# A trunk of two layers on one core: the opening in two parts of 512 features

## The chip, the cores and the metric

One core of a Trainium2 chip. The metric is device time in microseconds of one execution; three executions of the kernel before took 1212.24, 1216.07 and 1216.48 us, so the median is 1216.07. The engines are told by their plain names: TensorE (PE in the profile; PEld its weight loads), VectorE (DVE), ScalarE (ACT), GpSimd (POOL) and SyncE (SP), whose queue issues nearly all DMAs.

## The reference

A residual stream x of 256 tokens by 1024 features, float32, goes through two layers of three sub-layers. Each sub-layer takes a shift, a scale and a gate of 1024 features from one conditioning vector c, by c @ mod_w + mod_b, and computes

```
y = f(x * (1 + scale) + shift)
x = layer_norm(alpha * x + (1 + gate) * y)        # the feed-forwards enter with half the step
```

The first and the last sub-layer of a layer are feed-forwards, f(u) = (silu(u @ w_gate) * (u @ w_up)) @ w_down, with 2816 columns between; the middle one mixes tokens (sparse attention beside a gated delta rule in the first layer, latent attention in the second). Only the input of the first feed-forward, u = x * (1 + scale) + shift, and that feed-forward's first products are touched here.

## The kernel before, in words

All products that need float32 are made of three products of rounded parts: `split` (line 257) makes the high part on ScalarE (a cast, line 258) and the low part by a subtraction on VectorE or GpSimd (line 259); `mm3` adds high x high, high x low, low x high in PSUM (lines 263 to 265). u is kept transposed, features on partitions, as eight tiles of 128 features by 256 tokens, high and low.

The first feed-forward goes over 11 chunks of 256 of its 2816 columns. A chunk has two tiles of 128 columns; each needs a gate and an up product over all eight feature tiles, 96 matrix products per chunk. Behind chunk c come the down products of the two tiles of chunk c - 1 (12 products of 512 columns for each tile), so that TensorE has work while the silu of a chunk is made. Weights of a chunk come as two DMAs of 1 MB into tiles with the tag `w8` (three buffers); a down tile and a tile of modulation weights are 0.5 MB each with the tag `wd` (three buffers, shared). The low parts of the first eight down tiles are made on GpSimd (`load_down`, line 455), the rest on VectorE. `pace` draws modulation tiles in step with the chunks: from the fourth tile of columns on, those of the first gate (summed by VectorE, line 225, then over partitions by TensorE, line 180), then those of the next sub-layer.

The opening, ahead of the first chunk, has this order in SyncE's queue: c, the scale's weights (four DMAs of 1 MB), x (1 MB), the shift's weights (three of 1 MB, two of 0.5 MB), then the first chunk's gate and up weights in four pieces of 128 columns (512 bytes a row), then down tiles 0 and 1 and chunk 1. VectorE adds up weight rows times c over the eight row tiles (lines 218 and 225); TensorE sums over partitions by products with a column of ones (`mod_cols0`, line 147). One of the shift's eight tiles goes to TensorE directly. x is transposed by TensorE into PSUM as soon as it is there, and a few products with no use (`warm`) keep TensorE busy. When B, the shift with its bias, is there, VectorE and ScalarE make u pair by pair of feature tiles (`make_u`), and the first chunk's products follow in a written-out order of its parts (line 540). All of u needs all of the scale and the shift: 9 MB stand ahead of the first product.

The order of instructions on an engine is set by the tile framework: it follows the order of the program, but may take a later instruction first where it reckons that an earlier one is still waiting. `behind(...)` holds what is written in its block behind marked instructions of the same engines.

Of the kernel before, what the change touches and what calls it, by code (L numbers as in the profile page):

```python
# [30 lines left out]
HYBRID_LATE, LATENT_LATE = (1,), (5,)  # of these rows, the second block's products come last  # L31


class Trunk:
# [48 lines left out]
    def setup_bias(self):  # L83
        """the biases of shift and scale, as columns"""
# [36 lines left out]
    def warm(self, a):  # L121
        """keeps the PE array's clock up while nothing else can run on it"""
# [8 lines left out]
    def mod_cols(self, acc):  # L131
        """sum of acc over its partitions, [column % 128, column // 128]"""
# [9 lines left out]
    def mod_cols0(self, acc, c, use=None):  # L142
        """the same by products with c, which start earlier; use: takes two columns at a time"""
        pts = [self.bank("gu", (P, KD)) for _ in range(2 if use else 1)]
        for k in range(KD):
            pt = pts[k // 2 % len(pts)]
            self.last_col = self.nc.tensor.matmul(pt[:, k : k + 1], acc[:, k * P : (k + 1) * P], c,
                                                  start=True, stop=True)
            if use and k % 2:
                use(slice(k - 1, k + 1), pt)  # L150
        return pts[0]

    def mod_scale(self, si, sums):
# [4 lines left out]
        if si:  # L158
            l, j = self.subs[si - 1]
            o = (l * 3 + j) * KD  # L160
            nc.vector.tensor_tensor(out=B, in0=A, in1=self.pcol[:, 48 + o : 48 + o + KD], op=ALU.mult)
            nc.vector.tensor_tensor(out=A, in0=A, in1=self.pcol[:, o : o + KD], op=ALU.mult)
        self.AB[si] = [A, B]

    def mod_shift(self, si, acc):
# [3 lines left out]
        if si == 0:  # L169
            self.mod_cols0(acc, self.one[:, 0:1], lambda c, pt: add(B[:, c], pt[:, c], B[:, c]))  # L170
        else:
            add(B, B, b)
            add(B, B, self.mod_cols(acc))

    def mod_gate(self, si, acc, G):
        """G holds the bias"""
# [8 lines left out]
    def mod_gen(self):  # L185
        """(c @ mod_w + mod_b) of every sub-layer, in the order of use; partition sums come last; yields tiles loaded"""
        nc, t = self.nc, self.t
        self.AB, self.G = {}, {}
        todo = [(si, i, k) for si in range(len(self.subs)) for i in (1, 0, 2) for k in range(KD)]
        ws, loaded, G, step = {}, 0, None, None  # L190

        def load(si, i, k):
# [3 lines left out]
            if si or i == 2 or (i == 0 and k >= KD - 2):  # L196
                ws[si, i, k] = self.tl(self.wp, [P, D], "wd", bufs=3)
                nc.sync.dma_start(ws[si, i, k], src)
            elif k % 2 == 0:
                w2 = self.tl(self.wp, [P, 2, D], "w8", bufs=3)  # L200
                src = t["mod_w"][l, k * P : (k + 2) * P, off : off + D]
                nc.sync.dma_start(w2, src.rearrange("(q p) f -> p q f", p=P))
                ws[si, i, k], ws[si, i, k + 1] = w2[:, 0], w2[:, 1]

        for n, (si, i, k) in enumerate(todo):
            if k == 0:
                l, j = self.subs[si]
                off = (j * 3 + i) * D
                acc = self.tl(self.wp, [P, D], "G", bufs=2) if si == 0 and i < 2 else self.tl(self.wp, [P, D], "macc")
# [7 lines left out]
            if k == 0:  # L217
                nc.vector.tensor_scalar_mul(acc, w, c)
            elif (si, i, k) == (0, 0, 5):
                self.share = self.mod_cols0(w, c)  # L220
                with self.behind(self.last_col):
                    for _ in range(2):
                        self.warm(self.x[:, 0, 0:512])
            else:
                step = nc.vector.scalar_tensor_tensor(acc, w, c, acc, ALU.mult, ALU.add)  # L225
# [3 lines left out]
            self.mod_sums(si, i, acc, G, step)  # L229
            self.mdone.add((si, i))  # L230
            yield 0
            if si == 0 and i == 1:
                self.setup_bias()
                self.load_x()

    def mod_sums(self, si, i, acc, G, step):
        if i == 2:
            self.mod_gate(si, acc, G)
        elif i == 1:
            if si:  # L240
                self.mod_scale(si, self.mod_cols(acc))
            else:
                self.scale = self.mod_cols0(acc, self.one[:, 0:1])
        else:
            if not si:
                with self.behind(step):
                    self.mod_scale(si, self.scale)
                    self.nc.vector.tensor_tensor(out=self.AB[0][1], in0=self.share[:, 0:KD], in1=self.bcol[:, 0, 0],
                                                 op=ALU.add)
# [19 lines left out]
    def make_u(self, si, n, blocks):  # L269
        """n [P, NB, D] tokens on partitions -> uT = n * A + B, hi and lo [P, 2, KD, S]; blocks: one or all of them"""  # L270
        nc = self.nc
        if 0 in blocks:
            self.u = self.tl(self.wp, [P, 2, KD, S], "uT", F32R)
        u = self.u
        W = len(blocks) * P
        joint = len(blocks) > 1

        def rows(k0):
            pt = self.bank("acc" if joint else "gu", (P, 2, W))
            for q in range(2):  # L280
                for c, b in enumerate(blocks):
                    nc.tensor.transpose(pt[:, q, c * P : (c + 1) * P], n[:, b, (k0 + q) * P : (k0 + q + 1) * P],
                                        self.ident)
            return pt

        def affine(k0, pt):
            A, B = self.AB[si]
            ts = slice(blocks[0] * P, blocks[0] * P + W)
            if joint and k0 > 2:
                v = vs[:, k0 // 2 - 2]  # L290
            else:
                v = self.tl(self.wp, [P, 2, W], "tmp" if joint else "v", bufs=2 if joint else 3)
            for q, k in enumerate((k0, k0 + 1)):
                a, b = A[:, k : k + 1], B[:, k : k + 1]
                if q == 0 and (joint or blocks[0]):
                    nc.vector.tensor_scalar(v[:, q], pt[:, q], a, b, ALU.mult, ALU.add)
# [1206 lines left out]
```

## Time and profile before

| | |
|---|---|
| three executions | 1212.24, 1216.07, 1216.48 us |
| span of the profiled execution | 1212.3 us |
| TensorE busy | 1135.4 us, 94% |
| VectorE busy | 905.5 us, 75% |
| ScalarE busy | 547.6 us, 45% |
| GpSimd busy | 255.4 us, 21% |
| moved by DMA | 259.76 MB, 214 GB/s on the mean |

The span is the time from the first to the last instruction of one profiled execution; the profile gives no other time for that execution. Busy time of TensorE is modelled from pipelined matmuls, so that two products that start 0.12 us apart are each shown with 0.28 us; starts, not durations, tell its pace. A wait is put down to the engine that came last before the waiting instruction started.

### The profile page before, as it was taken

Reading aid. Unit: us, or ns where it says so; the run is one execution under the profiler, and the core shown is the slowest. Engines: PE = TensorE matmul, PEld = TensorE weight load, DVE = VectorE, ACT = ScalarE, POOL = GpSimd, SP = SyncE. Lnnn points to the kernel's source line nnn. Section 1 sums busy time; section 2 is a strip of 40 time slices with the busy share of each in tenths; the row PEclk is TensorE's granted clock in tenths of the full one; section 3 lists DMA queues with packets and bytes.
Section 4 is the critical chain, followed back from the end, with each engine's and each line's share of the span. In section 5 each row is a group of like instructions: output and inputs, shape, how many; then the busy total and the mean of one; then the engine's idle time right before and its main releaser. Section 6 shows DMA issues by size and latency. Waiting matters only on the chain.

```text
span 1212.3 us, 19687 instructions
## 1 busy us (share of the span) xinstructions
PE 1135.4 (94%) x7783; PEld 1035.5 (85%) x7783; DVE 905.5 (75%) x1376; ACT 547.6 (45%) x959; POOL 255.4 (21%) x186
## 2 busy tenths in 40 slices
PE   4998999999899998999999899899989998999997
PEld 3897999788787887989999889799978878899995
DVE  6699777698985677878885888778788438866545
ACT  0644444456433445533543543334456556544430
POOL 0631000224731452320000322000221234300001
PEclk9999999999999999999999999999999998999999
DMA  9779999454310586788997488889725135876620
GB/s 352 249 260 345 303 319 303 145 165 123 98 36 5 188 274 212 243 291 297 325 307 238 139 283 284 269 297 302 266 79 168 66 105 180 295 250 189 215 72 35
DMA packets 155334, 259.76 MB, mean 214 GB/s; under 512 B 8813, under 2 KB 117354, under 8 KB 155242
## 3 DMA queue, kind: packets, MB, share of 16 engines
q1 hardware_dynamic: 155050, 258.45, 63.9%
q8 instruction: 61, 1.00, 0.3%
q14 instruction: 31, 0.25, 0.1%
q10 hardware_dynamic: 192, 0.05, 0.0%
HBM read 257.43 MB, written 1.05 MB: 213 GB/s over the span
## 4 chain that ended last, share of the span: by engine, by line
PE 51%; DVE 22%; DMA 13%; ACT 5%; issue 5%; POOL 3%; SPq 0%; POOLq 0%; DVEq 0%; ACTq 0%
PE gu L265 8%; PE gu L264 8%; PE gu L263 7%; DMA wd<-ffn_w_down 7%; PE acc L265 6%; PE acc L263 6%; PE acc L264 6%; DVE macc L225 3%; DMA wd<-mod_w 3%; DMA w<-ffn_w_up 2%; DVE g L259 2%; POOL hd L259 2%; PE gu L732 2%; DVE u L259 2%; ACT hd L258 1%
## 5 line engine op out<-in xcount | busy, mean ns | idle before, releaser
L225 DVE SCALAR_TENSOR_TENSOR macc<-wd,csT,macc 128x1024 f32<-128x1024 f32 x112 | 169.0, 1509 | 27.1 <-DMA wd<-mod_w 26.5
L263 PE MATMUL gu<-uT,g 128*128 128x256 f32 x640 | 181.1, 283 | 1.4 <-ACT sg L548 1.4
L265 PE MATMUL gu<-uT,g 128*128 128x256 f32 x640 | 181.2, 283 | 1.2 <-DVE g L259 1.2
L265 PE MATMUL gu<-uT,u 128*128 128x256 f32 x640 | 181.2, 283 | 1.0 <-DVE u L259 1.0
L263 PE MATMUL gu<-uT,u 128*128 128x256 f32 x640 | 181.1, 283 | 0.0
L264 PE MATMUL gu<-uT,u 128*128 128x256 f32 x640 | 181.1, 283 | 0.0
L264 PE MATMUL gu<-uT,g 128*128 128x256 f32 x640 | 181.1, 283 | 0.0
L258 ACT CAST hd<-wd 128x1024 fp32r<-128x1024 f32 x88 | 92.2, 1049 | 136.8 <-DMA wd<-ffn_w_down 118.9
L263 PE MATMUL acc<-hd,h 128*128 128x512 f32 x352 | 141.3, 401 | 1.5 <-ACT h L258 1.5
L265 PE MATMUL acc<-hd,h 128*128 128x512 f32 x352 | 137.6, 391 | 1.1 <-DVE h L259 1.1
L264 PE MATMUL acc<-hd,h 128*128 128x512 f32 x352 | 137.7, 391 | 0.0
L259 DVE TENSOR_TENSOR g<-w,g 128x1024 fp32r<-128x1024 f32 x86 | 118.9, 1386 | 22.8 <-ACT g L258 22.3
L263 PEld LDWEIGHTS gu<-uT,g 128*128 128x128 f32 x640 | 122.7, 192 | 3.2 <-ACT sg L548 1.8
L265 PEld LDWEIGHTS gu<-uT,g 128*128 128x128 f32 x640 | 122.7, 192 | 1.6 <-DVE g L259 1.6
L264 PEld LDWEIGHTS gu<-uT,g 128*128 128x128 f32 x640 | 122.7, 192 | 1.4
L265 PEld LDWEIGHTS gu<-uT,u 128*128 128x128 f32 x640 | 122.9, 192 | 1.2 <-DVE u L259 1.2
L263 PEld LDWEIGHTS gu<-uT,u 128*128 128x128 f32 x640 | 122.9, 192 | 0.0
L264 PEld LDWEIGHTS gu<-uT,u 128*128 128x128 f32 x640 | 122.9, 192 | 0.0
L259 DVE TENSOR_TENSOR u<-w,u 128x1024 fp32r<-128x1024 f32 x81 | 104.1, 1290 | 24.5 <-ACT u L258 24.3
L258 ACT CAST u<-w 128x1024 fp32r<-128x1024 f32 (+1 forms) x89 | 91.6, 1039 | 62.7 <-DMA w<-ffn_w_up 51.9
L259 POOL TENSOR_TENSOR hd<-wd,hd 128x1024 fp32r<-128x1024 f32 x32 | 86.6, 2712 | 141.6 <-ACT hd L258 141.6
L259 POOL TENSOR_TENSOR hl<-w,hl 128x1024 fp32r<-128x1024 f32 x28 | 72.5, 2602 | 202.2 <-ACT hl L258 201.7
(392 smaller groups left out, 2495.2 us busy)
## 6 DMA issues: line engine op xcount, KB each, us to landing
wd<-mod_w SPq DMA_DIRECT2D x130, 512.0 KB, 4.8
wd<-ffn_w_down SPq DMA_DIRECT2D x88, 512.0 KB, 4.6
w<-ffn_w_gate SPq DMA_DIRECT2D x43, 1024.0 KB, 8.3
w<-ffn_w_up SPq DMA_DIRECT2D x43, 1024.0 KB, 6.9
w<-hyb_w_in SPq DMA_DIRECT2D x16, 1024.0 KB, 6.1
w<-mod_w SPq DMA_DIRECT2D x7, 1024.0 KB, 7.5
w<-hyb_w_out SPq DMA_DIRECT2D x4, 1024.0 KB, 4.9
w<-mla_w_out SPq DMA_DIRECT2D x4, 1024.0 KB, 5.4
```

Of the source, the lines that this page charges most:

```text
L225: step = nc.vector.scalar_tensor_tensor(acc, w, c, acc, ALU.mult, ALU.add)
L258: i = self.nc.scalar.copy(hi, src)
L259: return i, (eng or self.nc.vector).tensor_tensor(out=lo, in0=src, in1=hi.bitcast(F32), op=ALU.subtract)
L263: nc.tensor.matmul(out, lh, rh, start=first, stop=False)
L264: nc.tensor.matmul(out, lh, rl, start=False, stop=False)
L265: self.last_mm = nc.tensor.matmul(out, ll, rh, start=False, stop=last)
L732: nc.tensor.matmul(pt[:, b * S : (b + 1) * S], q[:, b * P : (b + 1) * P], k, start=True, stop=True)
```

## The change

The opening works on features 0 to 511 first, then on 512 to 1023. For each half: the scale's weights over these 512 columns (two DMAs of 1 MB, each with four row tiles), this half of x, the shift's weights over the same columns. The sums, the products with ones, the transposes of x, A, B and four tiles of u are made per half. Between the shift's two DMAs the weights of a chunk over this half's 512 features are loaded: chunk 0 in the first half, chunk 1 in the second. Behind the second half's sums both chunks' weights over features 512 to 1023 are loaded into tiles of `w8`. Products come in four blocks of 48: chunk 0 over the first half, chunk 1 over the first half, chunk 0 over the second, chunk 1 over the second. A chunk's four sums lie in two banks of PSUM, gate and up of a tile side by side; so both tiles of a chunk are complete together. Low parts of the weights are made on GpSimd, but for the gate's second halves (VectorE). TensorE's operations of the second half (the product with ones for the scale, the transposes) are held behind the first block of products. The first modulation tiles no longer pass through `mod_gen`, no tile of the shift goes to TensorE, the bias is fetched ahead of all, and of the warming products two are left. The first sub-layer's branch of `make_u` goes. In the feed-forward of the first sub-layer, chunks 0 and 1 take their products from `opening`. All else in the diff is names and comments.

```
+    def open(self, hf, after, first, second):
+        cols, ks = slice(hf * 512, hf * 512 + 512), slice(4 * hf, 4 * hf + 4)
+        A, B = self.AB[0]
+        for i in (1, 0):
+            acc = self.open_acc[i][:, cols]
+            for q in range(2):
+                if q and not i:
+                    first()
+                r = self.tl(self.wp, [P, 4, 512], "w8", bufs=3)
+                src = t["mod_w"][0, q * 512 : (q + 1) * 512, i * D + hf * 512 : i * D + hf * 512 + 512]
+                nc.sync.dma_start(r, src.rearrange("(q p) f -> p q f", p=P))
+                for k in range(4):
+                    c = self.cs[:, 4 * q + k : 4 * q + k + 1]
+                    if q or k:
+                        nc.vector.scalar_tensor_tensor(acc, r[:, k], c, acc, ALU.mult, ALU.add)
+                    else:
+                        nc.vector.tensor_scalar_mul(acc, r[:, k], c)
+            if i:
+                nc.sync.dma_start(self.x[:, :, cols], t["x"][0][:, cols].rearrange("(b p) d -> p b d", p=P))
             else:
+                second()
+            pt = self.bank("acc", (P, 4))
+            with self.behind(*after):
+                for k in range(4):
+                    nc.tensor.matmul(pt[:, k : k + 1], acc[:, k * P : (k + 1) * P], self.one[:, 0:1], start=True, stop=True)
+            if i:
+                nc.vector.scalar_tensor_tensor(A[:, ks], pt, 1.0, self.bcol[:, 0, 1, ks], ALU.add, ALU.add)
+                turned = []
+                for k0 in range(4 * hf, 4 * hf + 4, 2):
+                    px = self.bank("acc", (P, 2, S))
+                    turned.append((k0, px))
+                    with self.behind(*after):
+                        for q in range(2):
+                            for b in range(NB):
+                                nc.tensor.transpose(px[:, q, b * P : (b + 1) * P],
+                                                    self.x[:, b, (k0 + q) * P : (k0 + q + 1) * P], self.ident)
+                        if not hf:
+                            self.warm(self.x[:, 0, 0:512])
+            else:
+                nc.vector.tensor_tensor(out=B[:, ks], in0=pt, in1=self.bcol[:, 0, 0, ks], op=ALU.add)
+        for k0, px in turned:
+            v = self.tl(self.wp, [P, 2, S], "tmp", bufs=2)
+            nc.vector.tensor_scalar(v[:, 0], px[:, 0], A[:, k0 : k0 + 1], B[:, k0 : k0 + 1], ALU.mult, ALU.add)
+            nc.scalar.activation(v[:, 1], px[:, 1], AF.Identity, scale=A[:, k0 + 1 : k0 + 2], bias=B[:, k0 + 1 : k0 + 2])
+            self.marks[1:] = self.split(self.u[:, 0, k0 : k0 + 2], self.u[:, 1, k0 : k0 + 2], v)
...
+    def opening(self, wg, wu, gp):
...
+        def load(c, hf):
+            if hf:
+                both = self.tl(self.wp, [P, 2, 4, 256], "w8", bufs=3)
+            for g, w in enumerate((wg, wu)):
+                r = both[:, g] if hf else self.tl(self.wp, [P, 4, 256], "wd", bufs=3)
+                src = w[hf * 512 : hf * 512 + 512, c * 256 : (c + 1) * 256]
+                nc.sync.dma_start(r, src.rearrange("(k p) f -> p k f", p=P))
+                hls[c, hf, g] = hl = self.tl(gp, [P, 2, 4, 256], "gu"[g], F32R)
+                self.split(hl[:, 0], hl[:, 1], r, None if hf and not g else nc.gpsimd)
+
+        def products(c, hf):
+            if not hf:
+                pts[c] = [self.bank("gu", (P, 2, S)) for _ in range(2)]
+            for kp in (0, 2):
+                for q in range(3):
+                    for s in range(2):
+                        for g in range(2):
+                            for k in (kp, kp + 1):
+                                self.last_mm = nc.tensor.matmul(
+                                    pts[c][s][:, g], hls[c, hf, g][:, q // 2, k, s * P : (s + 1) * P], u[:, q % 2, 4 * hf + k],
+                                    start=not (hf or k or q or g), stop=hf == 1 and q == 2 and k == 3, skip_group_check=True)
+
+        self.setup_bias()
+        self.open(0, (), lambda: load(0, 0), lambda: None)
+        products(0, 0)
+        self.open(1, (self.last_mm,), lambda: load(1, 0), lambda: [load(0, 1), load(1, 1)])
+        products(1, 0)
+
+        def rest(c):
+            products(c, 1)
+            return {(s, g): pts[c][s][:, g] for s in range(2) for g in range(2)}
+
+        return rest
```

## Rows read from the trace of the kernel before

**Rows 1.** The page, part 4: shares by engine of the chain that ended last.

```profile
PE 51%; DVE 22%; DMA 13%; ACT 5%; issue 5%; POOL 3%; SPq 0%; POOLq 0%; DVEq 0%; ACTq 0%
```

**Rows 2.** TensorE's waits, 0 to 240: who waited for whom, us, times, longest us.

```profile
PE gu L147 <- DVE G L225: 15.0, 1, 15.0
PE gu L180 <- DVE macc L225: 4.2, 1, 4.2
...
PE gu L265 <- DVE g L259: 1.2, 1, 1.2
```

**Rows 3.** Timeline of the opening, all engines: start, duration (us), engine, line, count.

```profile
6.42 0.75 DVE L218 TENSOR_SCALAR G<-w,csT 128x1024 f32<-128x1024 f32 x1 [3.20 <-DMA w<-mod_w]
...
17.98 3.57 PE L147 MATMUL gu<-one,G 128*128 128x1 f32 x16 [14.96 <-DVE G L225]
...
25.87 0.34 PEld L147 LDWEIGHTS gu<-csT,w 128*128 128x128 f32 x1 [0.52 <-DMA w<-mod_w]
...
26.96 2.61 DVE L225 SCALAR_TENSOR_TENSOR G<-wd,csT,G 128x1024 f32<-128x1024 f32 x2
...
30.52 1.84 PE L147 MATMUL gu<-one,G 128*128 128x1 f32 x16
...
31.06 0.16 DVE L168 TENSOR_TENSOR B<-gu,B 128x2 f32<-128x2 f32 x1 [1.35 <-PE gu L147]
...
33.62 0.80 PE L540 MATMUL gu<-uT,g 128*128 128x256 f32 x2
```

**Rows 4.** Groups by line, 0 to 34: count, busy us, mean ns, idle before.

```profile
L225 DVE SCALAR_TENSOR_TENSOR G<-w,csT,G 128x1024 f32<-128x1024 f32 x11 | 14.1, 1285 | 2.4 <-DMA w<-mod_w 2.2
```

**Rows 5.** Timeline of TensorE: around 59.7, 64.9 and 76.4.

```profile
59.73 0.48 PE L265 MATMUL acc<-hd,h 128*128 128x512 f32 x1
...
64.86 0.28 PE L263 MATMUL gu<-uT,g 128*128 128x256 f32 x1
...
76.37 0.40 PE L263 MATMUL acc<-hd,h 128*128 128x512 f32 x1
```

**Rows 6.** Timeline of VectorE, 63 to 70.

```profile
63.66 2.36 DVE L259 TENSOR_TENSOR g<-w,g 128x1024 fp32r<-128x1024 f32 x2 [0.37 <-ACT g L258]
...
68.89 3.42 DVE L225 SCALAR_TENSOR_TENSOR macc<-wd,csT,macc 128x1024 f32<-128x1024 f32 x1
```

**Rows 7.** Timeline of SyncE's queue, 22 to 66.

```profile
54.64 0.33 SPq L198 DMA_DIRECT2D wd<-mod_w  x1
...
56.17 0.40 SPq L442 DMA_DIRECT2D w<-ffn_w_gate  x1
```

**Rows 8.** Waits of SyncE's queue, 20 to 70.

```profile
SPq L198 <- POOL hd L259: 8.2, 2, 6.5
```

**Rows 9.** Timeline of GpSimd, 36 to 70.

```profile
38.86 2.42 POOL L259 TENSOR_TENSOR g<-w,g 128x1024 fp32r<-128x1024 f32 x1 [1.47 <-ACT g L258]
...
51.21 5.76 POOL L259 TENSOR_TENSOR hd<-wd,hd 128x1024 fp32r<-128x1024 f32 x2 [4.03 <-ACT hd L258]
...
68.55 2.67 POOL L259 TENSOR_TENSOR hd<-wd,hd 128x1024 fp32r<-128x1024 f32 x1 [8.07 <-ACT hd L258]
```

**Rows 10.** Timeline of ScalarE, 61 to 64.

```profile
62.58 2.00 ACT L258 CAST g<-w 128x1024 fp32r<-128x1024 f32 x2 [1.74 <-DMA w<-ffn_w_gate]
```

**Rows 11.** Timeline of VectorE, 102 to 103.5.

```profile
102.64 0.68 DVE L182 SCALAR_TENSOR_TENSOR G<-gu,G 128x512 f32<-128x512 f32 x1
```

**Rows 12.** Stretches: length, busy us (x) of PE, PEld, DVE, ACT, POOL, clock, DMA, GB/s.

```profile
46.00:60.00 14.00, 12.80 (x104) 12.37 (x103) 8.92 (x9) 6.57 (x10) 6.94 (x3) 1.00 0.63 227
...
80.00:90.00 10.00, 8.98 (x67) 8.43 (x66) 9.96 (x11) 3.53 (x5) 6.23 (x35) 1.00 0.48 147
```

**Rows 13.** The same view, behind the wait of 4.2 us.

```profile
98.00:100.00 2.00, 1.01 (x2) 0.53 (x3) 1.86 (x4) 0.69 (x2) 0.00 (x0) 0.75 1.08 350
100.00:102.00 2.00, 2.00 (x5) 0.96 (x3) 0.91 (x2) 1.91 (x2) 0.00 (x0) 0.50 1.09 367
```

**Rows 14.** The same view, as the last modulation tiles and the first weights load.

```profile
24.00:26.00 2.00, 2.00 (x8) 1.48 (x7) 1.93 (x3) 0.00 (x0) 0.00 (x0) 1.00 1.04 416
...
28.00:30.00 2.00, 2.00 (x11) 1.38 (x11) 1.68 (x4) 0.12 (x1) 0.00 (x0) 1.00 1.21 291
```

More of the change, by code (lines that the diff above doesn't have):

```diff
@@ L218, in mod_gen @@
                 nc.vector.tensor_scalar_mul(acc, w, c)
[L219 to L223, printed above, removed]
             else:
-                step = nc.vector.scalar_tensor_tensor(acc, w, c, acc, ALU.mult, ALU.add)
+                nc.vector.scalar_tensor_tensor(acc, w, c, acc, ALU.mult, ALU.add)
             yield 1
@@ L239, in mod_sums @@
         elif i == 1:
[L240 to L243, printed above, removed]
-        else:
[L245 to L249, printed above, removed]
+            self.mod_scale(si, self.mod_cols(acc))
+        else:
             self.mod_shift(si, acc)
@@ L266, in mm3, with make_u @@
         return self.last_mm
-    def make_u(self, si, n, blocks):
+    def make_u(self, si, n, b):
         nc = self.nc
-        if 0 in blocks:
+        if b == 0:
             self.u = self.tl(self.wp, [P, 2, KD, S], "uT", F32R)
         u = self.u
[L275 to L279, printed above, removed]
+        A, B = self.AB[si]
+        ts = slice(b * P, (b + 1) * P)
+        for k0 in range(0, KD, 2):
+            pt = self.bank("gu", (P, 2, P))
@@ L280, in rows @@
             for q in range(2):
[L281 to L290, printed above, removed]
-            else:
[L292 to L296, printed above, removed]
-                else:
-                    nc.scalar.activation(v[:, q], pt[:, q], AF.Identity, scale=a, bias=b)
-            self.marks[1:] = self.split(u[:, 0, k0 : k0 + 2, ts], u[:, 1, k0 : k0 + 2, ts], v)
@@ L301, in make_u @@
-        if joint:
-            pts = [rows(k0) for k0 in range(0, KD, 2)]
-            vs = self.tl(self.wp, [P, 2, 2, W], "macc")
-            self.warm(n[:, 0, 0:512])
-            while self.count < 2 * KD:
-                self.count += next(self.bg)
-            next(self.todo[0])
-            self.need(si, 0)
-            with self.behind(self.last_col):
-                for _ in range(2):
-                    self.warm(n[:, 0, 0:512])
-            for k0 in range(0, KD, 2):
-                with self.behind(self.marks[1]):
-                    affine(k0, pts[k0 // 2])
-                if k0 < 4:
-                    with self.behind(self.marks[1]):
-                        self.marks[1:] = self.between[k0 // 2]()
-        else:
-            for k0 in range(0, KD, 2):
-                affine(k0, rows(k0))
@@ L527, in ffn @@
                 else:
-                    pts = {(s, g): self.bank("gu", (P, S)) for s in r2 for g in r2}
-                    if c:
+                    if c < 2 and not ahead:
+                        pts = part(c)
+                    else:
+                        pts = {(s, g): self.bank("gu", (P, S)) for s in r2 for g in r2}
                         for s in r2:
@@ L558, in ffn @@
                         load_down(i)
-                    with self.behind(*[part] if c == 1 else after):
+                    with self.behind(*[made] if c == 1 else after):
                         self.pace(max(0, i + 1 - skip) / (NT - 2 - skip))
@@ L562, in ffn @@
                 if c > 1 and self.left is not None:
-                    with self.behind(part):
+                    with self.behind(made):
                         next(self.left, None)
@@ L811, in run @@
         self.setup()
[L812 removed]
+        self.lead, self.count = 0, 2 * KD
+        self.AB, self.G, self.mdone = {}, {}, {(0, 0), (0, 1)}
         self.bg = self.mod_gen()
[L814 to L817 removed]
+        todo = [self.sublayer(si, l, j) for si, (l, j) in enumerate(subs)]
         self.rest = self.setup_rest()
```

115 lines of the change are left out of this document (35 added, 80 removed).

## The prediction

> **What bounds the kernel now.** I read the page first, then TensorE's waits, then the timeline of the opening engine by engine, then SyncE's queue. The chain that ended last is half TensorE [rows 1]: TensorE sets the pace nearly everywhere, and what it doesn't do while it waits is what the kernel can lose or win. Its waits in the first 240 us are few [rows 2]: one of 15.0 us at the very start, behind VectorE's sums of the modulation; one of 4.2 us for the sum of the first gate (line 180); some of 1 us. So the first feed-forward, once begun, runs from 33.62 us [rows 3] with hardly a gap, and the change touches only what lies ahead of that and the two chunks behind it. In the opening the transfers lead: the first megabyte is in at 6.42 us, the eighth (seven of mod_w, one of x) at 25.87 [rows 3], so 19.45 / 7 = 2.78 us a megabyte. VectorE sums at the same rate: two passes of 1.285 us a megabyte [rows 4], 2.6 us. The last sum ends at 29.57; the products of the shift's columns start at 30.52, behind warming products; the first two columns of B are done at 31.22; the first product of the feed-forward starts 2.40 us later [rows 3]. Chunk 1's products end at about 59.7, the rest of the first two down tiles takes until 64.86, and then chunk 2 starts [rows 5], just as its first low part is ready (63.66 + 2.36 / 2 = 64.8) [rows 6]. That is no accident of TensorE: chunk 2's gate weights were asked for only at 56.17, as the load of a modulation tile stood ahead of them in SyncE's queue until 54.64 [rows 7], and this waited up to 6.5 us for GpSimd's low part of a down tile [rows 8], which sits in the pair from 51.21 to 56.97 [rows 9]. The weights land at 62.58, 6.4 us after the request [rows 10].
>
> **The change, part by part.** MB n below is what SyncE's queue has moved by then, in its order of issue; it lands at 6.42 + 2.78 (n - 1).
>
> *Sums in halves.* The first half needs 2 MB of scale, 0.5 of x, 1 of shift, 1 of the first weights, 1 of shift: the sum's last tile is MB 5.5, in at 18.9 instead of MB 10. A pass over 512 columns is not in this stretch; from below it is half of 1.285 (0.64), from above 0.75, as a product-add over 512 from PSUM takes 0.68 [rows 11] and a chained pass starts a little later. I take 0.71, near that row: four passes are 2.8 us. All in all 28 such and four of 0.38 (half of 0.75, [rows 3]) are 21.4 us, against 13 of 1.285 and two of 0.75 before (one tile of the shift went to TensorE), 3.2 more; it gives back about as much, as three low parts of 1.2 us go from VectorE to GpSimd, and its idle time in 46 to 60 (5.1 of 14 us) covers the rest [rows 12].
>
> *Low parts on GpSimd.* The first half's two weight tiles (MB 4 and 4.5, in at 14.8 and 16.2, cast in 1.0 us each) have their low parts made on GpSimd, 2.42 us each at least [rows 9], exactly when VectorE sums. Beside such a pass VectorE stands still: a pass of 1.285 that began at 68.89 lasted 3.42, to 1.1 us past the end of GpSimd's of 68.55 to 71.22 [rows 6, 9]. So the second low part runs from 18.6 to 21.0, and the four passes behind MB 5.5 end at 23.8 instead of 21.7. Four columns on a cold TensorE cost 4 x 0.22 (3.57 / 16 at 17.98, against 1.84 / 16 at 30.52), B 0.16, and the 2.40 us from B to the first product as before: 27.3 (24.8 with neither price) against 33.62.
>
> *Products.* 96 take 76.37 - 64.86 = 11.5 us, so 0.12 each [rows 5], and a half of a chunk (48) 5.8. The warming products go but for two, and TensorE idles ahead of the first half: after the wait of 4.2 us the granted clock was 0.50, the lower level, for a stretch [rows 13], so I add 1.5 us (0 to 2). First half of chunk 0: 27.3 to 34.6. Then four columns and eight transposes for the second half (some 2.3 us) and the first half of chunk 1 (weights MB 10, in at 31.4): to 42.7. By then the second half of u is due: its last sum tile is MB 11, in at 34.2; GpSimd's low parts of MB 10 hold VectorE until some 35.9; sums 38.8, first product 41.8. The remaining 96 products run to 54.2, if the last weights (MB 13, in at 39.8) are split by 48.5; casts and low parts take some 5 us. That is 5.5 us ahead of before, and with the down tiles chunk 2 could start at 59.9, 5.0 ahead. What lies between 49.6 and 57 for the end of chunk 1 follows from the bounds above.
>
> *What is late next.* SyncE's order stays: down tiles 0 to 3, two modulation tiles, chunk 2. These small tiles share three buffers, now also with four of the first weights, so the second modulation tile again waits for the low part of down tile 2. GpSimd must first make two low parts of the second halves, the earlier from 38.1 (MB 12 and a cast), then those of down tiles 0, 1 and 2: five at 2.7 (2.42 alone, 2.88 in the pair at 51.21 [rows 9]) end at 51.6. The request goes 3.0 us earlier than at 54.64, and with the same steps behind it (landing, cast, low part) chunk 2 starts at 61.9 instead of 64.86; TensorE waits 2 us there. At 2.42 a pass the gain is 4.4, at 2.88 it is 2.1. SyncE issues two more DMAs than before for the same bytes, at about 0.4 us [rows 7] beside 2.78 a MB: nothing.
>
> *Behind chunk 2.* Between 60 and 99 VectorE is full (9.96 of 10 us from 80 to 90 [rows 12]); its work there starts with chunk 2's low parts, so it moves with them, the wait of 4.2 us stays, and TensorE, which has no other wait until the feed-forward ends, carries the 3.0 us on. The sum: -3.0 us on the profiled execution, whose span of 1212.3 is all that is known of its time, so 1209.3; that span equals the fastest of the three runs, 3.8 below their median, and by the median the forecast is 1213.
>
> *Rows of weights.* The loads of chunk 0 came in pieces of 512 bytes a row: the rate fell from 416 GB/s to 291 while they ran [rows 14]. The change reads 1 KB rows, which I priced at 2.78 us a MB, inside 2.5 and 3.6 (by these two rates). The Trainium skill's "DMA: Bandwidth & Descriptors" (Specifications) puts line rate at 512 bytes and above; the 291 here speaks against it at 512 itself. If its mark were right 1 KB rows could cost nothing extra, and the sum stays; if 1 KB is as slow as 512 bytes were here, MB 12 lands 2.5 us later and the gain falls to 0.5.
>
> **The rivals.** (a) *TensorE sets the pace.* If chunk 2's weights don't stand behind GpSimd (its passes short, or their request ahead of the modulation tile's), the gain is TensorE's own 5.0, and a VectorE that is ahead by then takes up to the 4.2 us wait and the slow clock behind it too: 5 to 10 us, about 1208.5. For it: VectorE's slack from 46 to 60. Against it: SyncE's queue kept its order before. (b) *Swallowed.* If VectorE comes to chunk 2 with a backlog of 3 us (halves at 0.75, more standing beside GpSimd) or the second half of products is put behind the second B on TensorE, which ends chunk 1 only at some 57, nothing is left: 1216. (c) *Slower.* Both tiles of a chunk now end together, so ScalarE's silu of chunk 1 comes only after 54. If the cast of down tile 2 stands behind it in ScalarE's order (GpSimd waited 4.03 us for that cast before, [rows 9]), its low part ends at 54.2 + 1.0 + 2.7 = 57.9 or later, the modulation tile goes at least 3.3 us later than before, TensorE waits over 8 us ahead of chunk 2 and has the lower clock for another 1 to 2: 4 to 6 us slower, 1221. It decides from the point where that low part ends behind 54.64.
>
> **How the numbers follow.** Forecast 0.43, (a) 0.29, (b) 0.16, (c) 0.12. The forecast's own range is 1211.5 to 1214.5 (gain 1.5 to 4.5); with most of (a) and (b) and no more than a fifth left out, 1206 to 1219. About 0.5%, 6 us, is what a measurement can tell from no change. Beyond it on the fast side lie two thirds of (a) and a few hundredths for an order of work later in the program that falls out better: 0.25. On the slow side a third of (c), the same few hundredths for a worse order, and as many for (b) and slow 1 KB rows together: 0.13. The rest, 0.62, is the same.
>
> **What would show it.** In the changed profile: the first product near 27 us, the last of chunk 1 near 54, the granted clock at the lower level in the first products; VectorE's half passes stretched beside GpSimd near 19 and 35; the request for the second modulation tile near 51.6 and chunk 2's first product near 62, with a TensorE wait of 1 to 3 us ahead of it; the gate's wait still about 4 us. Wrong if the first product comes behind 31, if the request for chunk 2's weights does not follow GpSimd's low part of down tile 2, or if the gate's wait goes: then VectorE, not the queue, was what I misjudged.

## The result, and the profile after

The changed kernel takes 1222.44 us (median of 9 runs, 1219.69 to 1225.7) against 1216.48 of the kernel before beside it: ratio 1.0053, 95% interval 1.0037 to 1.0069, some 6.4 us slower. The forecast was 1213.0. The profiled execution has a span of 1220.7 us; 1212.3 before.

Read first TensorE's waits, 0 to 240 us (engine, line, who was waited for: us, times, longest):

```profile
PE acc L279 <- DVE G L269: 8.9, 1, 8.9
PE gu L412 <- ACT uT L220: 7.8, 2, 4.8
...
PE gu L165 <- DVE macc L198: 4.6, 1, 4.6
```

Before there was one long wait and then the gate's [rows 2]. Now the wait for u comes twice, 2.99 and 4.81 us, once for each half. TensorE's timeline where the steps begin (start, duration, what ended the idle time in front):

```profile
30.25 0.58 PE L412 MATMUL gu<-uT,g 128*128 128x256 f32 x1 [2.99 <-ACT uT L220]
...
45.59 0.50 PE L279 MATMUL acc<-one,G 128*128 128x1 f32 x4
...
51.35 0.58 PE L412 MATMUL gu<-uT,g 128*128 128x256 f32 x1 [4.81 <-ACT uT L220]
...
71.42 0.28 PE L225 MATMUL gu<-uT,g 128*128 128x256 f32 x1
...
106.78 1.19 PE L165 MATMUL gu<-macc,one 128*128 128x512 f32 x1 [4.62 <-DVE macc L198]
```

The first product is 3.4 us earlier than before [rows 3] (1.9 by a second profile of the same opening, in before_ahead below: 32.13), the second half's first product (51.35) 9.5 us later than forecast. Chunk 2 starts 6.6 us later than in [rows 5], and the sum of the first gate comes at 106.78 in place of 98.99 (the wait of 4.2 us in [rows 2]): 7.8 us, and the span is 8.4 us longer. Why the second half is late is to be seen on VectorE (its timeline):

```profile
15.73 4.49 DVE L269 SCALAR_TENSOR_TENSOR G<-w,csT,G 128x512 f32<-128x512 f32 x3
20.48 4.84 DVE L269 SCALAR_TENSOR_TENSOR G<-w,csT,G 128x512 f32<-128x512 f32 x4 [0.26 <-DMA w<-mod_w]
...
31.59 5.12 DVE L269 SCALAR_TENSOR_TENSOR G<-w,csT,G 128x512 f32<-128x512 f32 x4
36.63 2.60 DVE L271 TENSOR_SCALAR G<-w,csT 128x512 f32<-128x512 f32 x1
...
40.85 3.90 DVE L269 SCALAR_TENSOR_TENSOR G<-w,csT,G 128x512 f32<-128x512 f32 x5
44.67 3.40 DVE L221 TENSOR_TENSOR g<-w,g 128x1024 fp32r<-128x1024 f32 x1
47.99 0.15 DVE L294 TENSOR_TENSOR B<-acc,bcol 128x4 f32<-128x4 f32 x1
```

and beside it on GpSimd:

```profile
17.33 2.35 POOL L221 TENSOR_TENSOR g<-wd,g 128x1024 fp32r<-128x1024 f32 x1 [16.04 <-ACT g L220]
19.63 2.79 POOL L221 TENSOR_TENSOR u<-wd,u 128x1024 fp32r<-128x1024 f32 x1
33.21 2.95 POOL L221 TENSOR_TENSOR g<-wd,g 128x1024 fp32r<-128x1024 f32 x1 [10.79 <-ACT g L220]
36.12 2.83 POOL L221 TENSOR_TENSOR u<-wd,u 128x1024 fp32r<-128x1024 f32 x1
44.45 2.53 POOL L221 TENSOR_TENSOR u<-w,u 128x1024 fp32r<-128x1024 f32 x1 [5.50 <-ACT u L220]
...
53.21 10.37 POOL L221 TENSOR_TENSOR hd<-wd,hd 128x1024 fp32r<-128x1024 f32 x4
```

Four half passes undisturbed take 3.1 us (the five from 40.85 took 3.90); beside GpSimd's low parts three took 4.49, four took 4.84 and 5.12, and the first pass of a tile 2.60 in place of 0.48. Then the low part of w_gate (44.67, itself standing beside GpSimd's pass of 44.45) goes ahead of the add that makes the second B. The queue of SyncE waits for all this (its waits, 0 to 66 us):

```profile
SPq L265 <- DVE G L269: 9.9, 3, 5.5
SPq L400 <- DVE G L269: 9.7, 2, 5.8
SPq L476 <- POOL hd L221: 7.4, 1, 7.4
SPq L265 <- DVE G L271: 4.5, 1, 4.5
...
SPq L181 <- POOL hd L221: 3.9, 2, 2.4
```

It waited 24.1 us in six places for VectorE to give weight buffers back, where the kernel before waited 11.5 in five: VectorE led the transfers, not the other way round. The second shift's last tile shows it best: it was asked for at 30.50, no DMA moved anything from 36 to 37 (188 GB/s from 35 to 36), so it was in by 36, and VectorE came to it with the last four of the five passes from 40.85, at about 41.6. And the chain of [rows 7 to 9] is there again, later (SyncE's timeline): second modulation tile 61.24 (54.64 before), chunk 2's weights 63.85 (56.17).

```profile
61.24 0.33 SPq L181 DMA_DIRECT2D wd<-mod_w  x1
...
63.85 0.40 SPq L460 DMA_DIRECT2D w<-ffn_w_gate  x1
```

TensorE's granted clock was at the lower of its two levels (0.50) in two stretches that follow idle time (columns as in [rows 12]; the clock is the third figure from the right):

```profile
30.00:34.00 4.00, 3.75 (x17) 3.75 (x18) 3.89 (x7) 2.18 (x4) 0.79 (x1) 0.50 1.08 368
...
50.00:54.00 4.00, 2.23 (x9) 1.94 (x9) 2.96 (x3) 4.00 (x6) 3.14 (x2) 0.50 0.35 139
```

### The profile page after: what moved, and what is told of

It is laid out like the page before. It is cut to its first block, busy times and chain, and to the rows that moved or that the text cites. A ratio compares the mean times of both kernels' runs of the same rounds, so it can differ in the third digit from the quotient of the medians.

```text
span 1220.7 us, 19651 instructions
## 1 busy us (share of the span) xinstructions
PE 1133.1 (93%) x7761; PEld 1033.2 (85%) x7761; DVE 913.7 (75%) x1388; ACT 547.4 (45%) x957; POOL 262.0 (21%) x187
## 4 chain that ended last, share of the span: by engine, by line
PE 51%; DVE 23%; DMA 13%; issue 5%; ACT 5%; POOL 3%; SPq 0%; POOLq 0%; DVEq 0%; ACTq 0%
PE gu L227 8%; PE gu L226 8%; PE gu L225 8%; PE acc L227 6%; DMA wd<-ffn_w_down 6%; PE acc L225 6%; PE acc L226 6%; DVE macc L198 3%; DMA wd<-mod_w 3%; DMA w<-ffn_w_up 2%; PE gu L724 2%; DVE g L221 2%; POOL hd L221 2%; ACT hd L220 1%; DVE x L356 1%
## 5 line engine op out<-in xcount | busy, mean ns | idle before, releaser
L227 PE MATMUL gu<-uT,u 128*128 128x256 f32 x624 | 176.8, 283 | 1.5 <-DVE u L221 1.5
L225 PE MATMUL gu<-uT,g 128*128 128x256 f32 x624 | 176.6, 283 | 0.5 <-ACT sg L540 0.5
L227 PE MATMUL gu<-uT,g 128*128 128x256 f32 x624 | 176.7, 283 | 0.0
L226 PE MATMUL gu<-uT,u 128*128 128x256 f32 x624 | 176.6, 283 | 0.0
L225 PE MATMUL gu<-uT,u 128*128 128x256 f32 x624 | 176.6, 283 | 0.0
L226 PE MATMUL gu<-uT,g 128*128 128x256 f32 x624 | 176.6, 283 | 0.0
L225 PEld LDWEIGHTS gu<-uT,g 128*128 128x128 f32 x624 | 119.6, 192 | 2.4 <-ACT sg L540 1.0
L227 PEld LDWEIGHTS gu<-uT,u 128*128 128x128 f32 x624 | 119.7, 192 | 1.9 <-DVE u L221 1.9
L226 PEld LDWEIGHTS gu<-uT,g 128*128 128x128 f32 x624 | 119.6, 192 | 1.4
L225 PEld LDWEIGHTS gu<-uT,u 128*128 128x128 f32 x624 | 119.7, 192 | 0.0
L226 PEld LDWEIGHTS gu<-uT,u 128*128 128x128 f32 x624 | 119.7, 192 | 0.0
L227 PEld LDWEIGHTS gu<-uT,g 128*128 128x128 f32 x624 | 119.6, 192 | 0.1
L220 ACT CAST u<-w 128x1024 fp32r<-128x1024 f32 x86 | 89.4, 1048 | 60.7 <-DMA w<-ffn_w_up 48.8
L221 DVE TENSOR_TENSOR u<-w,u 128x1024 fp32r<-128x1024 f32 x78 | 97.2, 1251 | 19.9 <-ACT u L220 19.9
```

The lines of the kernel that those rows point to most:

```text
L220: i = self.nc.scalar.copy(hi, src)
L221: return i, (eng or self.nc.vector).tensor_tensor(out=lo, in0=src, in1=hi.bitcast(F32), op=ALU.subtract)
L225: nc.tensor.matmul(out, lh, rh, start=first, stop=False)
L226: nc.tensor.matmul(out, lh, rl, start=False, stop=False)
L227: self.last_mm = nc.tensor.matmul(out, ll, rh, start=False, stop=last)
```

## The experiments

My theory was T1: VectorE sets the pace of the opening, and its passes stand while GpSimd makes low parts. Rivals: T2, chunk 2's weights behind GpSimd's low parts in SyncE's queue; T3, TensorE's lower clock; T4, the order in VectorE's and ScalarE's queues; T5, transfers; later ones are named where they come. Each run is read at the sum of the first gate in its profile, beside its ratio to the kernel before: from there to the end of the span the kernel before needs 1113.3 us, the changed one 1113.9, so what is lost ahead of it reaches the end. Each profile is one execution, and a difference under some 2 us between two of them shows nothing by itself: half_sums below, with a ratio of 0.9996, has its gate's sum 2.3 us ahead of the kernel before. Intervals are of the time ratios.

**Low parts on VectorE.** The six in the opening leave GpSimd.

```
-  self.split(hl[:, 0], hl[:, 1], r, None if hf and not g else nc.gpsimd)
+  self.split(hl[:, 0], hl[:, 1], r)
```

> The changed kernel, with the low parts of the first two chunks' weights (six tiles) made on VectorE instead of GpSimd. Theory 1 (VectorE sets the opening's pace: its half-wide sums, and GpSimd's six passes of 2.4 to 2.9 us, 15.8 in all, beside which it stands): six passes of 1.2 us take the place of some 10 to 12 us of standing, so the second B comes 4 to 5 us earlier than 48.0, chunk 1's products end near 61 instead of 65.4, and the time falls by 4 to 5 us to about 1218. Theory 2 (the queue: chunk 2's weights stand behind GpSimd's low parts of the down tiles): the opening's end does not matter by itself, the time falls only as far as the request for chunk 2's weights (63.85) moves. Theory 3 (the clock: TensorE starts its blocks at the lower clock): no change of more than 1 us.

Ratio 1.0049 (1.0031 to 1.0067), gate's sum 103.89. VectorE's groups to there, of this kernel and then of the changed one:

```profile
L269 DVE SCALAR_TENSOR_TENSOR G<-w,csT,G 128x512 f32<-128x512 f32 x28 | 21.0, 750 | 1.0 <-DMA w<-mod_w 0.2
...
L271 DVE TENSOR_SCALAR G<-w,csT 128x512 f32<-128x512 f32 x4 | 1.9, 484 | 5.4 <-DMA w<-mod_w 5.4
```

```profile
L269 DVE SCALAR_TENSOR_TENSOR G<-w,csT,G 128x512 f32<-128x512 f32 x28 | 26.9, 962 | 1.0 <-DMA w<-mod_w 0.3
...
L271 DVE TENSOR_SCALAR G<-w,csT 128x512 f32<-128x512 f32 x4 | 4.1, 1014 | 4.2 <-DMA w<-mod_w 4.2
```

So standing beside GpSimd costs the sums 31.0 - 22.9 = 8.1 us. Yet only 2 us of it reach the second half's first product (49.32), and the time shows no gain over the changed kernel (1.0049 beside 1.0053): theory T1 alone falls short.

**No low parts at all.** The six low parts are not computed: ScalarE writes a second copy of the weights in their place.

```
+  nc.scalar.copy(hl[:, 0], r)
+  nc.scalar.copy(hl[:, 1], r)
```

> The changed kernel, but the low parts of the first two chunks' weights are not computed: ScalarE writes a second copy of the weights in their place, so neither VectorE nor GpSimd works on them. Theory 1: the lock is gone and no pass takes its place; second B near 38 to 40, chunk 1's products end near 55 to 57, the time falls by 8 to 10 us to about 1213, a few us below the kernel before or level with it. Theory 2: GpSimd is free for the down tiles from the start, so the gain would be as large, but then with chunk 2's request early and the second B unmoved. Theory 3: under 1 us.

Ratio 1.0035 (1.0024 to 1.0047), gate's sum 102.2: 4.6 us ahead of the changed kernel's, 2.2 by the ratios, where T1 expected 8 to 10. The last sum ended at 40.6, but the second half's first product came at 47.99: the columns came only at 42.81, behind block (1,0), and u behind ScalarE's four copies from 41.83 on (its activation at 46.42).

**Down tiles' low parts on VectorE**, tiles 0 to 3.

```
-  ... nc.gpsimd if i < 8 else None)
+  ... nc.gpsimd if (0 if first != "start" else 4) <= i < 8 else None)
```

> The changed kernel, with the low parts of down tiles 0 to 3 of the first feed-forward on VectorE instead of GpSimd. Theory 2: the second modulation tile is asked for at about 55 to 57 instead of 61.2, chunk 2's weights follow, and the time falls by 4 to 5 us. Theory 1: chunk 1's products still end at 65.4 (within 1 us), chunk 2 can't start before 71, and the time stays within 1.5 us of the changed kernel's 1222.4. Theory 3: no change.

Ratio 1.0054 (1.0037 to 1.0072), gate's sum 103.70. The modulation tile went out at 57.05, not 61.24; the trace gained 3.1 us, the times show none of it. The profiled execution was the fastest of the six (1218.84 us), so the 3.1 may be its own. Neither the six low parts alone nor these four alone gain any time that can be told from none.

**More warming products** (15: eight beside the first half's transposes, seven behind the products with ones for B) in the opening.

> The changed kernel with eleven more products without use on TensorE around the first half's transposes and behind the two products with ones for B, to have the clock up when the blocks start. Theory 3: the first block takes 5.8 us instead of 7.8 and the third block is 2 us shorter; chunk 1 ends 2 to 4 us earlier, time down by as much, to about 1219. Theory 1: the first block's two microseconds don't count, since the third waits for the second B; the third's do: about 2 us at most, 1220.5. Theory 2: none, as chunk 2's weights come no earlier.

Ratio 1.0079 (1.0062 to 1.0097), gate's sum 105.99. All theories missed the time. T3's blocks did get shorter: block (0,0) took 6.4 us in place of 7.9, the second half's two blocks 11.9 in place of 13.8. But the warming products themselves kept TensorE from the second half until 52.16 (four of them, shown as eight records, took 5.38 us from 47.35 on, at a clock of 0.52 from 48 to 50). So the lower clock costs some 1.5 to 2 us at each of the two places; whether that reaches the end is left open.

**Order of the second half's low parts**: behind the split of u.

> Only the order: the casts of the four second-half weights stay, their low parts are held until u's second half is split. Theory T4 (what stands ahead of the second shift on VectorE and ScalarE): the second shift's add no longer stands behind the 3.40 us low part of w_gate (before it at 47.99), so block (0,1) starts near 48.9 in place of 51.35, chunk 2 at 69.0 and the gate's sum at 104.4 in place of 106.78: about 2.4 us less, +4 us on the kernel before. Theory T1 (VectorE's total work paces, whatever the order): the same work in another order, gate's sum within 0.8 us of 106.78.

Ratio 1.0063 (1.0039 to 1.0087), gate's sum 107.41. The add went ahead, but the columns came 2.5 us later (48.05). The four passes from 31.68 that end the second scale's sums took 7.15 us, TensorE waited 1.16 us for the last of them (its columns at 38.98 in place of 38.12), its granted clock was 0.63 in 40 to 42 and 0.52 in 42 to 44, and so the transposes and block (1,0) ran slowly. What the order alone is worth can't be read from this run.

**Chunk 1's first weights later**, behind the second shift's last tile.

```
-  self.open(1, ..., lambda: load(1, 0), lambda: [load(0, 1), load(1, 1)])
+  self.open(1, ..., lambda: None, lambda: [load(1, 0), load(0, 1), load(1, 1)])
```

> Chunk 1's first-half weights (1 MB) are asked for behind the last tile of the second shift, not ahead of it, so their products come behind its column products. Theory T5 (transfers and TensorE's order set the second half): the last tile lands some 2.8 us earlier, the columns don't wait for block (1,0), and (1,0) runs while u's second half is made: no TensorE idle of 4.8 us ahead of (0,1), which starts near 47.5; gate's sum near 103. Theory T1 (VectorE paces the sums, and stands beside GpSimd's low parts): the sums end at most 1 to 2 us earlier (the two low parts of chunk 1 no longer beside them); (0,1) near 49.5, gate's sum near 105.

Ratio 1.009 (1.0066 to 1.0113), gate's sum 109.35. The second shift's last tile was asked for at about 30.6, as before (30.50), since it waits for a buffer that VectorE holds; the columns came at 46.25, no earlier than 45.59. A megabyte less ahead of them did not bring the columns forward: transfers don't pace the second half (T5 falls). Why the whole is longer by some 4.5 us than the changed kernel was not followed up.

**Half of the sums on TensorE**, in two versions.

```
+  for r, q, c in late:
+      nc.tensor.matmul(pt[:, k : k + 1], r[:, q, k * P : (k + 1) * P], c, start=False, stop=q == 3)
```

> Three things at once: half of the opening's sums (rows 512 to 1023 of every part) as column products on TensorE straight from the weights, all low parts of the opening and of down tiles 0 to 3 on VectorE, and the second half's low parts behind the split of u. T1 with T4 (VectorE's sums, its standing beside GpSimd, and the order are all of the loss): VectorE loses some 11 us of sums, none of its passes stands, second shift near 41.5, (0,1) near 45.5, gate's sum near 99.5; time within 1 us of the kernel before. T5 (transfers, and block (1,0) ahead of the second shift's columns): (0,1) not ahead of 47.5, gate's sum near 101.5, +2.5 us.

> combo with chunk 1's first-half weights behind the last tile of the second shift. T1 with T5 (both): second shift near 39.5, block (1,0) beside the making of u's second half, (0,1) near 46 with TensorE idle for less than 2 us ahead of it, gate's sum near 98 to 99.5, time 0 to 1 us below the kernel before. If T5 is nothing: as combo. If TensorE's 20 column products a part (some 2.4 us each) are the new bound: gate's sum 1 to 2 us behind combo's.

Ratios 1.0148 (1.012 to 1.0176) and 1.0176 (1.015 to 1.0203). Gate's sums 118.93 and 122.54. Each column of sums (one product with ones and four with c) took 1.1 us, and 2.1 at the lower clock, not the 0.6 assumed; in combo SyncE then waited 22.6 us in three places for buffers that TensorE held. A new bound; nothing about T1 follows.

**Half passes alone, in the kernel before.**

```
+  for hs in (slice(0, 512), slice(512, D)) if si == 0 and i < 2 else (slice(0, D),):
+      step = nc.vector.scalar_tensor_tensor(acc[:, hs], w[:, hs], c, acc[:, hs], ALU.mult, ALU.add)
```

> The kernel before with one part of the change alone: each pass of the opening's sums made in two halves of 512 columns; tiles, transfers, products as they were. By the passes of the run with all low parts on VectorE (0.75 and 0.48 us a half), 26 and 4 halves take 21.4 us where the 13 and 2 whole passes took 18.2. If VectorE sets the pace of the opening (T1): the first product comes 2 to 3 us later than 33.62, the gate's sum near 101, time +2 us. If the transfers set it and VectorE has slack (what the prediction took): only the passes behind the last tile count, +0.2 to 0.6 us, no difference that can be measured.

Ratio 0.9996 (0.9987 to 1.0006), gate's sum 96.72: halving costs nothing that can be measured here. But its passes alternate between the two halves, 0.66 us apart, where the change's chain on one half, 0.79 apart (last section), so it tests the halving in a milder form.

**Queues mended, nothing on GpSimd.** The two moves of low parts above, and: the second scale's add behind the last pass on VectorE; the second shift's columns in the middle of block (1,0); what belongs to the second half's weights, but for chunk 0's casts, behind the split of u.

```
+  with self.behind(step):
+      nc.vector.scalar_tensor_tensor(A[:, ks], pa, 1.0, self.bcol[:, 0, 1, ks], ALU.add, ALU.add)
...
+  products(1, 0, (0,))     # ahead of the columns
+  products(1, 0, (2,))     # behind them
```

> All low parts of the opening and of down tiles 0 to 3 on VectorE, and three stands taken out of queues: the second scale's add goes behind the last pass of the second shift on VectorE (it stood 2.45 us there, waiting for columns that TensorE makes behind block (0,0)); the second shift's columns go into the middle of block (1,0) on TensorE; on ScalarE and VectorE everything of the second half's weights but chunk 0's casts goes behind the split of u. T7 (once VectorE and GpSimd don't stand for each other, what is left is these three queues): last sum near 41.1 in place of 43.6, shift's add 42.2, block (0,1) near 45 to 45.5 with TensorE idle under 1 us ahead of it and its clock not fallen, chunk 2 near 64, gate's sum 97.5 to 99.5, time -1.5 to +1 us on the kernel before. T6 (the loss goes on behind the opening: chunk 2's weights, modulation tiles, GpSimd): block (0,1) early all the same, but gate's sum not under 102, +3 us.

Ratio 0.9995 (0.9984 to 1.0005), gate's sum 99.05: T7, in its own numbers. VectorE's timeline:

```profile
38.15 3.11 DVE L269 SCALAR_TENSOR_TENSOR G<-w,csT,G 128x512 f32<-128x512 f32 x4
41.17 0.15 DVE L303 SCALAR_TENSOR_TENSOR A<-acc,bcol 128x4 f32<-128x4 f32 x1
42.40 0.16 DVE L304 TENSOR_TENSOR B<-acc,bcol 128x4 f32<-128x4 f32 x1 [1.07 <-PE acc L283]
```

From 30 to 64 us TensorE has no wait. The row of the granted clock shows full speed throughout, though the first products, until 33.2, start 0.21 us apart and only then 0.12.

**Queues mended, low parts on GpSimd.**

> The same three queues mended, the low parts where the change has them (five on GpSimd in the opening, down tiles 0 to 3 on GpSimd too). T7: VectorE's passes stand again beside GpSimd's (some 5 to 8 us of VectorE in the opening), last sum near 44, block (0,1) near 47.5, and the down tiles' low parts hold SyncE's requests: gate's sum 102 to 104, +3 to +5 us. If standing is hidden once the queues are mended (T8): gate's sum within 1 us of the other run's.

Ratio 1.006 (1.0046 to 1.0074), gate's sum 105.82, beyond even T7's 102 to 104 and +3 to +5 us; standing is not hidden (T8 falls). One stretch of seven sums on VectorE, 5.5 us undisturbed:

```profile
37.35 9.59 DVE L269 SCALAR_TENSOR_TENSOR G<-w,csT,G 128x512 f32<-128x512 f32 x7
```

**Nothing on GpSimd, queues as the change has them**: the two moves of low parts alone.

> The missing corner: all low parts of the opening and of down tiles 0 to 3 on VectorE, the queues as the change has them (with low parts on GpSimd and queues as they are the gate's sum was at 106.78, with the queues alone mended 105.82, with both mended 99.05). T7 (both causes, the queues only bite once nothing stands): block (0,1) near 49.3 as with the opening's low parts alone, gate's sum 101 to 102.5, time +2 to +4 us on the kernel before. If standing beside GpSimd is the whole loss and the queues nothing: gate's sum 99 to 99.5, no difference from the kernel before. If the queues are what mattered and standing little: gate's sum not under 103.5, +5 us.

Ratio 1.0017 (1.0004 to 1.0031), gate's sum 102.15: T7's numbers. VectorE's timeline shows two of the queues:

```profile
37.69 0.16 DVE L281 SCALAR_TENSOR_TENSOR A<-acc,bcol 128x4 f32<-128x4 f32 x1 [2.87 <-PE acc L279]
...
45.52 0.16 DVE L294 TENSOR_TENSOR B<-acc,bcol 128x4 f32<-128x4 f32 x1 [0.58 <-PE acc L279]
45.60 1.23 DVE L221 TENSOR_TENSOR u<-w,u 128x1024 fp32r<-128x1024 f32 x1
46.75 0.54 DVE L297 TENSOR_SCALAR tmp<-acc,A,B 128x256 f32<-128x256 f32 x1
47.20 1.21 DVE L221 TENSOR_TENSOR g<-w,g 128x1024 fp32r<-128x1024 f32 x1
```

The four corners, gate's sum and ratio:

| | queues as they are | queues mended |
|---|---|---|
| low parts on GpSimd | 106.78, 1.0053 | 105.82, 1.0060 |
| on VectorE | 102.15, 1.0017 | 99.05, 0.9995 |

Moving ten low parts (six of the opening, four of down tiles) off GpSimd gives back 4.6 and 6.8 us at the gate's sum, about 4.4 and 7.9 us by the ratios. Mending the queues gives back 3.1 us (2.7 by the ratios) once nothing is on GpSimd; before that 1.0 us in the profiles and nothing in the ratios, so no gain is shown. The corners don't part two ways in which GpSimd can cost time: VectorE's standing, and the later requests in SyncE's queue (the modulation tile at 61.24, at 57.05 with the four down tiles' low parts off GpSimd, at 56.56 with all ten).

**Chunk 2's weights asked for earlier**, behind down tile 2, in the mended kernel and in the kernel before.

```
+  if first == "start" and i == 2:
+      early[2] = fetch(2)
```

> The repaired change (nothing on GpSimd, three queues mended), and chunk 2's gate and up weights asked for behind down tile 2, ahead of down tile 3 and the modulation tiles. In the repaired run chunk 1's products ended at 56.8, 2.9 us ahead of the kernel before, but chunk 2's first product still came at 64.43 (before 64.86): its weights were asked for at 55.16 and cast at 63.33. T9 (SyncE's order alone takes the 3 us, as the prediction's step on the modulation tile has it): the cast comes before 60, chunk 2 follows the down tiles without a wait near 62.4 to 63, gate's sum near 97, time 1.5 to 2.5 us below the kernel before. T10 (VectorE, full from 70 to the gate's sum, takes it anyway): chunk 2 early, gate's sum 98.5 to 99.5 with a longer wait of TensorE there (6 us), no difference.

> The kernel before with the same one move (chunk 2's weights asked for behind down tile 2, ahead of down tile 3 and the modulation tiles). There TensorE reached chunk 2 without a wait, so T9 and T10 both expect chunk 2's first product at 64.9 as before, and no difference beyond 1 us; if it is 2 us faster, what the other run gains has nothing to do with the opening in two parts.

Mended: 0.9991 (0.998 to 1.0002), gate's sum 97.86, no difference that can be measured. The cast came at 53.57, as T9 had it, but TensorE made 38 down products first and reached chunk 2 only at 65.05, so neither T9 nor T10 was put to the test. Kernel before: 0.9981 (0.9966 to 0.9996), gate's sum 95.16, 3.8 us earlier, of which 1.5 are there at the first product already (32.13 for 33.62), ahead of the move; 2.3 us (0.5 to 4.1) by the ratio, without the opening in two parts, which neither theory expected.

## Why the prediction was wrong

*The step that failed* is "By then the second half of u is due: its last sum tile is MB 11, in at 34.2; ... sums 38.8, first product 41.8": transfers were taken to lead and VectorE to follow, at a price of 2.1 and 1.7 us for standing. Measured: the tile in by 36, but the last sum at 44.67 and the first product at 51.35. Of these 9.55 us, 5.87 had gathered by the last sum; the other 3.68 lie between it and the first product (6.68 us where 3.0 were forecast).

- *VectorE's extra 3.2 us*: the sums took 31.0 us against 18.2 before (the group of [rows 4], 2.6 and 1.5 us): 12.8 more. 4.7 of them come from the half passes and the one tile more, 8.1 from standing beside GpSimd. The pass was priced nearly right (0.71; it is 0.75 long, and four follow 0.79 apart). What failed is the standing: the row that shows it [rows 6, 9] was used for two low parts of the first half and some 1.7 us of the second, where four stood beside sums and two more beside VectorE's own passes.
- *Slack.* 5.1 idle us from 46 to 60 [rows 12] were set against work that fell in 20 to 48, where VectorE is busy 25.7 of 28 us.
- *Three stands in queues* were not counted: columns behind block (1,0), about 0.9 us, the add of B behind w_gate's low part, about 1.4, u's cast behind w_up's, about 0.9.
- *Transfers*: 2.78 us a megabyte was right. From 39 to 40 only 1 KB rows of chunk 0 were under way, at 383 GB/s; the Trainium skill's "DMA: Bandwidth & Descriptors" (Specifications), line rate from 512 bytes, agrees with it there, though not with the 291 of [rows 14].
- *First product*: 30.25 for 27.3. The last sum of the first half ended at 25.32 for 23.8 (standing, 1.5 us); the columns took 1.87 for 0.88 us (1.0), as the row of 3.57 us [rows 3] shows each of its eight columns as two records, so a column costs 0.45 and not 0.22; the rest lies behind B. With low parts on VectorE it came at 28.67.
- *Cold clock in the first products*: 7.9 us measured for block (0,0), 7.3 forecast.
- *Chunk 2 behind GpSimd's chain and the modulation tile*: the mechanism held, at 61.24 in place of 51.6.
- *The gate's wait stays*: 4.6, and 3.2 to 6.4 in all runs. The three signs of being wrong that the prediction named (a first product behind 31, a request that doesn't follow GpSimd's low part, no wait for the gate) all stayed away: they look ahead of the place that failed and behind it.
- *What an earlier chunk 1 is worth*: mended, its products ended at 56.8, 2.9 us ahead of before (59.7), but only 1.4 ahead of the same point in before_ahead's profile (58.2), and chunk 2 started at 64.43 (64.86 before), as its weights were asked for at 55.16, behind two modulation tiles, and cast at 63.33. With that request ahead too, chunk 2 started at 65.05, behind more down products, and the gate's sum at 97.86 can't be told from 98.99; VectorE is nearly full from 70 us to there in both (26.9 of 28 us to 98, with the request ahead), which no run took away.

Rival (b) named VectorE's backlog, but priced it at 3 us and at no loss. Rival (c) had the right sign, and close to the size, by luck, from another place: GpSimd made the four low parts from 53.21 on without a gap, so no cast held it up; it was late before.

The Trainium skill's "SBUF — State Buffer" (Who interferes with whom) says that VectorE shares a pair of ports with GpSimd, that tensor_scalar can take the pair, and that a VectorE instruction with two inputs in SBUF contends with a GpSimd instruction that reads SBUF. The trace agrees: the pass at 36.63 (tensor_scalar) took 2.60 in place of 0.48 us and ended 0.3 us behind GpSimd's of 36.12, and the 28 sums (two inputs in SBUF) took 962 ns each beside GpSimd's low parts and 750 without.

What the runs show together: the loss is gone (0.9995) when ten low parts leave GpSimd and three queues are mended; the queues alone give no gain (1.0060), the low parts alone leave 1.0017, just clear of no loss. What stays open: how the loss parts between VectorE's standing and the later requests in SyncE's queue, how much of the lower clock's cost reaches the end, and whether an earlier end of chunk 1, 1.4 to 2.9 us in the mended kernel, is too small to measure or is lost behind it.

## What to carry to other kernels

Before work goes to GpSimd, list VectorE's passes that fall beside it, each one, and charge the standing to the stage in which they fall, and don't set it against idle time of another. When an input is cut in two so that products can start early, every add and column product between the parts can stand in an in-order queue behind the first part's work: place them by hand. And an earlier start is not yet a gain: here 1.4 to 2.9 us at the end of chunk 1 gave none that could be measured, even with the next request moved ahead too.

## What was not expected of the hardware

- Half passes that alternate between the halves of an accumulator follow 0.66 us apart (12 in 8.04 us, the last 0.74 long), those that chain on one half 0.79 (4 in 3.11): the difference between the two kernels is that the chained pass needs the result of the one in front of it, which fits the 0.12 us more, though no run changes that alone. Two alternating halves, 1.33, cost what a chained whole pass does (three in 3.93, so 1.32). VectorE's timeline, halves alone in the kernel before:

```profile
9.04 8.04 DVE L227 SCALAR_TENSOR_TENSOR G<-w,csT,G 128x512 f32<-128x512 f32 x12 [0.62 <-DMA w<-mod_w]
```

- A float32 product of 128 x 128 by one column shows as two records, so counting records as columns halves its price: four columns of ones took 1.87 us in the changed kernel (x8 below), at a granted clock of 0.50, and eight took 1.84 us at full clock [rows 3], so 0.45 and 0.23 each. Products with c cost the same in combo: groups of one product with ones and four with c took 1.09 us at full clock (starts at 40.43 and, three groups later, 43.70), 0.22 each, and 2.13 at the lower (53.59, 55.72), 0.43 each. TensorE's timeline, first of the changed kernel, then of combo:

```profile
25.38 1.87 PE L279 MATMUL acc<-one,G 128*128 128x1 f32 x8 [8.91 <-DVE G L269]
```

```profile
40.43 0.28 PE L281 MATMUL acc<-one,G 128*128 128x1 f32 x2
40.58 1.03 PE L283 MATMUL acc<-csT,w 128*128 128x1 f32 x8
```
